# Retention mixer's entry: a written order for VectorE and ScalarE, and the values' first weight tiles requested ahead of the sums

## The chip, the cores and the metric

One NeuronCore of a Trainium2 chip runs the whole program. The metric is device microseconds of one execution. The core's engines run side by side, each through its own in-order list of instructions, and semaphores hold an instruction until its operands are there: TensorE (PE) multiplies, VectorE (DVE) and ScalarE (ACT) work on tiles of 128 partitions, GpSimd (POOL) and SyncE (SP) issue DMA transfers here, POOL those that add to what already lies in the tile.

## The reference, cut to what matters

The program is a two-layer encoder for 512 tokens of width 1024: layer 0 mixes with window and neighbourhood attention, layer 1 with retention, each followed by an MLP. The change lies at the start of layer 1's mixer:

```python
def _odd_mixer(x, norm_g, w_in, dec_f, dec_b, gn_g, w_out):
    B, S, _ = x.shape
    h = _rmsnorm(x, norm_g)
    q, k, v, g = _split(h @ w_in, ODD_SPLITS)      # 1024, 1024, 2048, 2048 columns
    q = q.reshape(B, S, RET_HEADS, RET_DK)
    k = k.reshape(B, S, RET_HEADS, RET_DK) * (RET_DK ** -0.5)
    v = v.reshape(B, S, RET_HEADS, RET_DV)
    ...
```

All of it is float32.

## The kernel before

**Precision.** A float32 operand is split into a high part (a cast, on ScalarE) and a low part (operand minus high part, on VectorE). A product is three matmuls: high by high, high by low, low by high. So every weight tile of 128x1024 (512 KB, asked for by a DMA on SP's queue) costs one cast on ScalarE and one subtraction on VectorE before TensorE can finish with it. In `load_w` (L130 on) these are L165 and L166, the tiles are called `wraw`, `whi`, `wlo`.

**The entry of the retention mixer** works on `xg`, the transposed input times the norm's gain. The division by the root mean square is done at the end, since it is a factor per token: `rq_*`, a few 128x4 operations, give it in `tok_r`; `wide` (L1691) spreads it, four transposes on TensorE (L1698) turn it, and ScalarE copies it to `rstd_b` (L1699). `deviations` holds these, and `proj_a` calls it by a hook in its second half.

`project` for the first quarter of the heads does, in this order: `proj_a` for q (two weight tiles, 48 matmuls of 512 columns), `values.combine(0)` to `(3)`, `proj_a` for k (two tiles), the start of the values. Evacuating q or k is one multiplication by `rstd_b` (VectorE, to `tmp`), a cast `qh`/`kh` (ScalarE, L1710) and a subtraction `ql`/`kl` (VectorE, L1711).

**The values** (class `Projections`, a `Strassen`) are blocked 2x2 and use seven products instead of eight, with sums of weight blocks and of input blocks. Each product is cut in two steps x = 0, 1 of one weight tile and 12 matmuls (L1509 to L1511), so steps 0 and 1 multiply by the weight block A11, steps 2 and 3 by S1 = A21 + A22, steps 4 and 5 by S2 = A11 + S1 (the addition is `sum2`, on VectorE, L1079, in place in A11's tile), steps 6 and 7 by A12, 8 and 9 by S3, and so on. `combine(i)` makes the input's combinations for a pair i of row blocks: `row` (the input by its gain, ScalarE, L1005), four operations of 256 columns to `c` (VectorE, L1011 to L1014), a cast `uh` (ScalarE, L1017) and a subtraction `ul` (VectorE, L1018). Steps 2 to 5 read all four, two in x = 0 and two in x = 1. `high(k)` and `low(k)` (L1101, L1107) make a step's weight parts, called `shi`/`slo` for every third step and `whi`/`wlo` for the others.

**Requests.** `request` asks on SP's queue for a plain block (L1074) or for the first addend of a sum (L1070); for a sum POOL then issues a second DMA that adds the second addend (L1072), once the first has landed. `ask(a, b)` issues the requests planned for steps a to b - 1. A11 and the sums share a pool of six tiles `sraw`; block combinations alternate between a tile `c` of their own and one of these.

**Order.** In the stream of steps (`stream`, two steps ahead: product of k, early calls, `high(k + 2)`, calls of `mid[k]`, `low(k + 2)`, calls of `post[k]`), DVE, ACT and PE run in the order in which the code is written (`tc.manual_schedule`). Before the stream, in `project`, a scheduler of the compiler sets each engine's order from its own estimate and from `high_priority` and `issue_after`.

Of the kernel before, what the change touches and what calls it, by code (L numbers as in the profile page):

```python
# [9 lines left out]
F32 = mybir.dt.float32  # L10
F32R = mybir.dt.float32r
AF = mybir.ActivationFunctionType
ALU = mybir.AluOpType
# [3 lines left out]
P = 128  # L17
# [15 lines left out]
def hybrid_encoder_kernel(  # L33
# [18 lines left out]
    nc = tc.nc  # L52
    mm = nc.tensor.matmul
    act = nc.scalar.activation
    V = nc.vector
# [113 lines left out]
    def proj_a(w, r0, nk, c0, xs, evac, hook=None):  # L169

        ps = [acc(), acc()]
        chunks = {}

        def weights(kb):
            if kb not in chunks:
                rows = slice(r0 + kb * P, r0 + min(kb + 4, nk) * P)
                chunks[kb] = load_w([w[rows, c0 : c0 + 256]], 4)
            return chunks[kb]

        for k, m in [(k, m) for k in range(nk) for m in range(2)]:  # L180
            if hook is not None and (k, m) == (4, 0):
                hook(0)
            hi, lo = weights(k - k % 4)
            if hook is not None and (k, m) == (4, 0):
                hook(1)
            xh, xl = xs[k]
            cs = slice(m * P, (m + 1) * P)
            mm(ps[m], hi[:, k % 4, cs], xh, start=k == 0, stop=False)  # L188
            mm(ps[m], hi[:, k % 4, cs], xl, start=False, stop=False)  # L189
            mm(ps[m], lo[:, k % 4, cs], xh, start=False, stop=k == nk - 1)  # L190
        for m in range(2):
            evac(m, ps[m])
# [770 lines left out]
    class Strassen:  # L963
# [17 lines left out]
        READS2 = ((0, 0, 1), (1, 1, -1), (0, 1, 1), (0, 0, 1), (1, 1, -1), (0, 1, 1), (1, 0, -1))  # L981
        KEPT = ("kept", "sq", "rstd_b", "sq")
        SB = 4
        CB = (("sraw", 6),)

        def __init__(self, pool, w1, w2, norm, last):
            self.pool, self.w, self.w2, self.norm, self.last = pool, w1, w2, norm, last
            self.raw, self.parts, self.ins = {}, {}, {}
            self.steps, self.base = [], {}
            for q in range(4):  # L990
                if q:
                    for u in (2 * q, 2 * q + 1):
                        self.base[1, u] = len(self.steps)
                        self.steps += [(1, u, j, 0) for j in range(7)]
                self.base[2, q] = len(self.steps)
                self.steps += [(2, q, j, x) for j in range(7) for x in range(2)]
            self.early, self.mid, self.post, self.asked = ({} for _ in range(4))
            self.hid, self.val, self.rows, self.ps = {}, {}, {}, {}
            self.requests()

        def combine(self, i):

            pool, norm = self.pool, self.norm
            y = self.tmp()
            act(y, xT[2 * i], AF.Copy, scale=norm.gain(2 * i))  # L1005
            b11, b12 = y[:, :256], y[:, 256:]
            x21, x22 = xT[2 * i + 1][:, :256], xT[2 * i + 1][:, 256:]
            g, ng = norm.gain(2 * i + 1), norm.minus_gain(2 * i + 1)
            tag, bufs = self.CB[i % len(self.CB)]
            c = pool.tile([P, 4, 256], F32, tag=tag, bufs=bufs, name="c")  # L1010
            V.tensor_tensor(c[:, 0], b11, b12, op=ALU.subtract)  # L1011
            V.scalar_tensor_tensor(c[:, 1], x22, ng, c[:, 0], op0=ALU.mult, op1=ALU.subtract)
            V.scalar_tensor_tensor(c[:, 2], x22, g, b12, op0=ALU.mult, op1=ALU.subtract)
            V.scalar_tensor_tensor(c[:, 3], x21, ng, c[:, 1], op0=ALU.mult, op1=ALU.subtract)  # L1014
            h = pool.tile([P, 4, 256], F32R, tag=f"uh{i}", name="uh")
# [41 lines left out]
        def block(self, kind, u, name, x):  # L1057
# [3 lines left out]
            r, c = u * 1024 + j * 512 + x * 256, i * 512  # L1061
            return self.w2[r : r + 256, c : c + 512].rearrange("(k p) c -> p k c", p=P)

        def request(self, kind, u, name, x):
            pl, tag, bufs = (wpool, "wraw", 3) if name in ("A12", "A22") else (self.pool, "sraw", 6)
            t = pl.tile([P, 1024], F32, tag=tag, bufs=bufs, name=tag)
            v = t[:].rearrange("p (k c) -> p k c", k=4 if kind == 1 else 2)
            self.raw[kind, u, name, x] = v
            if name[0] == "S":
                self.asked_last = nc.sync.dma_start(v, self.block(kind, u, "A21", x)).ins  # L1070
                second = self.block(kind, u, "A22" if name == "S1" else "A11", x)
                G.dma_start(v, second, accum_op=ALU.add)  # L1072
            else:
                nc.sync.dma_start(v, self.block(kind, u, name, x))  # L1074

        def sum2(self, kind, u, x=0):

# [371 lines left out]
    class Projections(Strassen):  # L1449
# [2 lines left out]

        CB = (("c", 1), ("sraw", 6))

        def __init__(self, pool, row, tiny, w, norm, done, rb, gates):
            self.pool, self.tiny, self.w, self.norm, self.done = pool, tiny, w, norm, done
            self.rb, self.gates = rb, gates
            self.tmp = row  # L1460
            self.raw, self.parts, self.ins, self.rows, self.ps = {}, {}, {}, {}, {}
# [201 lines left out]
    def odd_mixer(norm, next_norm):  # L1663
# [4 lines left out]
        late, marks = [], []  # L1668
# [6 lines left out]
        G.memset(gn_eps, GN_EPS)  # L1675

        delta = pool.tile([P, 896], F32, name="delta")
        nc.scalar.dma_start(delta, delta_d)

        rc = tok_r[:, 0]  # L1680
        rb = stat.tile([P, S], F32, tag="rstd_b", name="rstd_b")
# [1 line left out]

        def deviations(part):

            if part:
                values.ask(-99, -8)
                return
            rsqrt_small(rc, mean_square(), NB, tiny)
            wide = stat.tile([P, S], F32, tag="sq", bufs=2, name="wide")  # L1690
            V.tensor_copy(  # L1691
                wide[:].rearrange("p (t m) -> p t m", t=NB),
                rc.unsqueeze(2).to_broadcast([P, NB, P]),
            )
            pt = aux()
            for t in range(NB):
                ts = slice(t * P, (t + 1) * P)
                nc.tensor.transpose(pt[:, ts], wide[:, ts], ident)  # L1698
            nc.scalar.copy(rb, pt)  # L1699
# [7 lines left out]
        def split(src, tag, bufs, half=half):  # L1707
            h = half(tag + "h", bufs)
            l = half(tag + "l", bufs)
            marks.append(nc.scalar.copy(h, src).ins)  # L1710
            V.tensor_tensor(l, src, h.bitcast(F32), op=ALU.subtract)  # L1711
# [8 lines left out]
        class Quarter:  # L1720
# [7 lines left out]
            def project(self):  # L1728
# [12 lines left out]
                    )  # L1741
                    self.k[m] = split(t, "k", 2)

                hook = None if qt else deviations
                mark = marks[-1] if qt else None
                proj_a(w_in_o, 0, 8, qt * 256, xg, ev_q, hook)
                if qt == 0:
                    values.combine(0)
                    values.combine(1)
                    values.ask(-99, -5)  # L1750
                    values.combine(2)
                    values.combine(3)
                first_sums = values.asked_last if qt == 0 else None
                with tc.issue_after(first_sums) if qt == 0 else ExitStack():
                    proj_a(w_in_o, 0, 8, 1024 + qt * 256, xg, ev_k)
                if qt == 0:
                    values.scales(rc)
                    values.ask(-2, 1)
                    values.ask(-5, -2)
                    values.enter()  # L1760
                    return
                with tc.issue_after(mark):
                    self.load_gates(nc.scalar)

            def load_v(self):
                self.back = []
# [116 lines left out]
        with tc.tile_pool(name="odd_values", bufs=1) as first:  # L1883
# [7 lines left out]
                rb,  # L1891
                gates,
            )
            quarters[0].project()
# [137 lines left out]
```

## Time and profile before

| | us |
|---|---|
| time, median of 3 runs (lowest to highest) | 1296.97 (1296.62 to 1297.88) |
| profiled execution, its own time | 1298.3 |
| its span on the core | 1296.5 |
| PE busy | 1270.2 |
| DVE busy | 1055.6 |
| ACT busy | 824.8 |
| mean granted TensorE clock | 0.996 of full speed |

The span is what the trace covers; the time is a little longer. Busy time is a share over the whole program, so it tells which engine the rest is measured by, not what a single place costs. In timeline rows the first figure is the start in us from the span's start, the second the length; several instructions of a kind in a row are one line with xN; a bracket gives the idle time before it and what ended it. Tiles are named without numbers there.

### The profile page before, as it was taken

The numbers are of one execution on the slowest core, as the hardware profiler recorded it, in microseconds if no ns is written. First come the engines' busy times: TensorE is split into PE (matmuls) and PEld (weight loads), VectorE is DVE, ScalarE is ACT, GpSimd is POOL, SyncE is SP. The second block draws the span as 40 slices with busy tenths as digits, with TensorE's granted clock in tenths as the row PEclk, the third lists the DMA queues.
The fourth block names the chain that finished last, engine by engine and source line by source line (L and its number), as shares of the span: only waits on it lengthen the run. The fifth ranks groups of instructions, "written<-read, shape, count | busy, mean of one in ns | idle before, by whom it ended". The sixth has DMA issues, their size and how long they took to land.

```text
span 1296.5 us, 19409 instructions
## 1 busy us (share of the span) xinstructions
PE 1270.2 (98%) x7186; PEld 1115.6 (86%) x7186; DVE 1055.6 (81%) x1603; ACT 824.8 (64%) x1382; POOL 160.9 (12%) x167
## 2 busy tenths in 40 slices
PE   8999999999999999988999999999999999999998
PEld 7888978888989899866899988888888889898997
DVE  6788887879797988967888789877776788979888
ACT  4789875775756757564775575463546757466573
POOL 0222430010520111011111000000000111101100
PEclk9999999999999999998999999999999999999999
DMA  5323322668696787167899343424135787867862
GB/s 170 97 74 87 100 66 77 192 165 203 169 205 168 179 220 170 50 196 173 214 284 237 108 137 114 130 68 128 49 98 165 176 215 176 201 172 179 211 148 81
DMA packets 167071, 196.15 MB, mean 151 GB/s; under 512 B 12224, under 2 KB 124864, under 8 KB 166976
## 3 DMA queue, kind: packets, MB, share of 16 engines
q1 hardware_dynamic: 130384, 147.74, 36.9%
q0 software_dynamic: 27776, 37.75, 17.9%
q10 hardware_dynamic: 8816, 9.41, 2.3%
q8 instruction: 56, 0.92, 0.3%
q14 instruction: 39, 0.32, 0.1%
HBM read 184.39 MB, written 10.49 MB: 150 GB/s over the span
## 4 chain that ended last, share of the span: by engine, by line
PE 88%; DVE 5%; ACT 3%; DMA 2%; issue 1%; POOL 0%; ACTq 0%; SPq 0%; DVEq 0%
PE acc L1299 7%; PE acc L1315 7%; PE acc L1316 7%; PE acc L1314 7%; PE acc L1300 7%; PE acc L1301 7%; PE acc L189 6%; PE acc L188 6%; PE acc L190 6%; PE acc L1510 2%; PE acc L1511 2%; PE acc L1509 2%; PE aux L1820 1%; PE aux L1821 1%; PE aux L1822 1%; PE aux L1315 1%
## 5 line engine op out<-in xcount | busy, mean ns | idle before, releaser
L1101 ACT CAST whi<-sraw 128x1024 fp32r<-128x1024 f32 x121 | 126.8, 1049 | 82.0 <-PE acc L1316 25.2
L1107 DVE TENSOR_TENSOR wlo<-sraw,whi 128x1024 fp32r<-128x1024 f32 x121 | 147.8, 1222 | 34.0 <-ACT whi L1101 33.5
L165 ACT CAST whi<-wraw 128x1024 fp32r<-128x1024 f32 (+2 forms) x83 | 78.5, 946 | 77.5 <-PE acc L189 44.6
L166 DVE TENSOR_TENSOR wlo<-wraw,whi 128x1024 fp32r<-128x1024 f32 (+2 forms) x74 | 82.6, 1116 | 38.7 <-ACT whi L165 37.8
L1072 POOL DMA_DIRECT2D sraw<-in_w_mlp_out_dram x32 | 38.7, 1251 | 597.7 <-DMA sraw<-in_w_mlp_out_dram 411.4
L188 PE MATMUL acc<-xh,whi 128*128 128x512 f32 x272 | 106.3, 392 | 0.0
L189 PE MATMUL acc<-xl,whi 128*128 128x512 f32 x272 | 105.9, 389 | 0.0
L190 PE MATMUL acc<-xh,wlo 128*128 128x512 f32 x272 | 105.8, 389 | 0.0
L1299 PE MATMUL acc<-uh,whi 128*128 128x256 f32 x344 | 97.9, 285 | 0.4 <-ACT s L1190 0.3
L1300 PE MATMUL acc<-ul,whi 128*128 128x256 f32 x344 | 97.3, 283 | 0.0
L1301 PE MATMUL acc<-uh,wlo 128*128 128x256 f32 x344 | 97.3, 283 | 0.0
L1101 ACT CAST shi<-sraw 128x1024 fp32r<-128x1024 f32 x59 | 62.0, 1050 | 49.1 <-PE acc L1316 10.7
L1107 DVE TENSOR_TENSOR slo<-sraw,shi 128x1024 fp32r<-128x1024 f32 x59 | 72.1, 1222 | 19.4 <-ACT shi L1101 19.0
L1268 DVE SCALAR_TENSOR_TENSOR rows<-acc,tok_r,rows 128x512 f32<-128x512 f32 (+1 forms) x97 | 71.5, 740 | 1.9 <-PE acc L1316 1.9
L1107 DVE TENSOR_TENSOR wlo<-wraw,whi 128x1024 fp32r<-128x1024 f32 x46 | 56.2, 1221 | 15.0 <-ACT whi L1101 15.0
L1299 PEld LDWEIGHTS acc<-uh,whi 128*128 128x128 f32 x344 | 66.0, 192 | 1.2 <-ACT s L1190 1.2
L1300 PEld LDWEIGHTS acc<-ul,whi 128*128 128x128 f32 x344 | 66.0, 192 | 0.0
L1301 PEld LDWEIGHTS acc<-uh,wlo 128*128 128x128 f32 x344 | 66.0, 192 | 0.0
L190 PEld LDWEIGHTS acc<-xh,wlo 128*128 128x128 f32 x272 | 51.1, 188 | 10.8
L189 PEld LDWEIGHTS acc<-xl,whi 128*128 128x128 f32 x272 | 51.1, 188 | 10.4
L188 PEld LDWEIGHTS acc<-xh,whi 128*128 128x128 f32 x272 | 51.1, 188 | 10.4
L1101 ACT CAST whi<-wraw 128x1024 fp32r<-128x1024 f32 x46 | 48.3, 1050 | 11.4 <-PE acc L1316 9.0
(400 smaller groups left out, 4180.3 us busy)
## 6 DMA issues: line engine op xcount, KB each, us to landing
sraw<-in_w_mlp_out_dram SPq DMA_DIRECT2D x48, 512.0 KB
wraw<-in_w_mlp_in_dram SPq DMA_DIRECT2D x40, 512.0 KB
sraw<-in_w_mlp_in_dram SPq DMA_DIRECT2D x36, 512.0 KB
sraw<-in_w_mlp_out_dram POOLq DMA_DIRECT2D x32, 512.0 KB, 8.7
wraw<-in_w_mlp_out_dram SPq DMA_DIRECT2D x32, 512.0 KB
wraw<-in_w_in_o_dram SPq DMA_DIRECT2D x32, 512.0 KB
sraw<-in_w_mlp_in_dram POOLq DMA_DIRECT2D x24, 512.0 KB, 8.2
sraw<-in_w_in_o_dram SPq DMA_DIRECT2D x24, 512.0 KB
```

The source lines that it names most:

```text
L166: eng.tensor_tensor(lu, used, hu.bitcast(F32), op=ALU.subtract)
L188: mm(ps[m], hi[:, k % 4, cs], xh, start=k == 0, stop=False)
L189: mm(ps[m], hi[:, k % 4, cs], xl, start=False, stop=False)
L190: mm(ps[m], lo[:, k % 4, cs], xh, start=False, stop=k == nk - 1)
L1101: nc.scalar.copy(h, self.weight(k))
L1107: V.tensor_tensor(l, self.weight(k), h.bitcast(F32), op=ALU.subtract)
L1299: mm(o, h[:, i, cs], bh, start=st, stop=False, skip_group_check=True)
L1300: mm(o, h[:, i, cs], bl, start=False, stop=False, skip_group_check=True)
L1301: mm(o, l[:, i, cs], bh, start=False, stop=i == 3, skip_group_check=True)
L1314: mm(oc, bh[:, i, cs], hc, start=st, stop=False, skip_group_check=True)
L1315: mm(oc, bh[:, i, cs], lc, start=False, stop=False, skip_group_check=True)
L1316: mm(oc, bl[:, i, cs], hc, start=False, stop=end, skip_group_check=True)
```

## The change

The entry of the first quarter gets a function of its own, `project_first`, whose VectorE and ScalarE instructions are issued in the written order. `combine` is split in three (`gained`: the row; `combined`: the four operations; `combined_parts`: the cast and the subtraction), all four blocks use one tile `c`, and the three pieces are placed one by one. `deviations` runs in q's second half from `part` 2; A11 is asked for by its hook at q's second tile (`part` 3), after `raw_tile` has taken the tiles for S1. A12, S3 and so on follow k. k's casts and subtractions go into `mid[2]` and `mid[3]` of the stream, block 3 into `post[0]`, and the decay distances `delta` (448 KB) are asked for on SP's queue in step 4's `early` calls instead of on ACT's queue.

```diff
         for k, m in [(k, m) for k in range(nk) for m in range(2)]:
-            if hook is not None and (k, m) == (4, 0):
-                hook(0)
+            if hook is not None and (k, m) in ((0, 0), (4, 0)):
+                hook(2 * (k // 4))
             hi, lo = weights(k - k % 4)
-            if hook is not None and (k, m) == (4, 0):
-                hook(1)
+            if hook is not None and (k, m) in ((0, 0), (4, 0)):
+                hook(2 * (k // 4) + 1)
...
+        def gained(self, i):
+            self.y[i] = self.tmp()
+            act(self.y[i], xT[2 * i], AF.Copy, scale=self.norm.gain(2 * i))
...
-        CB = (("c", 1), ("sraw", 6))
+        CB = ("c", 1)
...
-        nc.scalar.dma_start(delta, delta_d)
...
-            if part:
-                values.ask(-99, -8)
+            if part < 2:
+                return
+            if part == 3:
+                for x in range(2):
+                    values.raw_tile(2, 0, "S1", x)
+                for x in range(2):
+                    values.request(2, 0, "A11", x)
                 return
...
+                def between(step):
+                    if step == 0:
+                        values.combined(0)
+                    elif step == 2:
+                        values.combined_parts(0)
+                        values.combined(1)
+                        for m in range(2):
+                            part("q", m)
+                        for m in range(2):
+                            parts("q", m)
+
+                proj_a(w_in_o, 0, 8, 0, xg, keep("q"), deviations)
+                E = mybir.EngineType
+                with tc.manual_schedule(engines={E.DVE, E.Activation}):
+                    for i in range(4):
+                        values.gained(i)
+                    with tc.issue_after(values.asked_last):
+                        proj_a(w_in_o, 0, 8, 1024, xg, keep("k"), between)
+                    values.ask(-99, -7)
...
+                    values.scales(rc)
+                    values.ask(-2, 1)
+                    values.ask(-7, -2)
+                    values.combined_parts(1)
+                    values.high(0)
+                    values.low(0)
+                    values.combined(2)
+                    values.high(1)
+                    values.low(1)
+                    values.combined_parts(2)
+                    for m in range(2):
+                        part("k", m)
+
+                def rest():
+                    values.combined(3)
+                    values.combined_parts(3)
+
+                values.post.setdefault(0, []).append(rest)
+                values.mid.setdefault(2, []).append(lambda: parts("k", 0))
+                values.mid.setdefault(3, []).append(lambda: parts("k", 1))
+                values.early.setdefault(4, []).append(lambda: nc.sync.dma_start(delta, delta_d))
```

What the queues and engines then hold, in three places. In the rows stand line, operation, result and operands; the numbers behind the names tell one tile from another.

SP's queue behind q's two weight tiles, before: S1's first addends (L1070), k's tiles (L144), A12 (L1074, `wraw`), A11 (L1074, `sraw`), A22, S3.

```order
L1070 DMA sraw_6243<-in_w_in_o_dram 128x2x512
L1070 DMA sraw_6246<-in_w_in_o_dram 128x2x512
L144 DMA wraw_6335<-in_w_in_o_dram 128x4x256
L144 DMA wraw_6365<-in_w_in_o_dram 128x4x256
L1074 DMA wraw_6410<-in_w_in_o_dram 128x2x512
L1074 DMA wraw_6412<-in_w_in_o_dram 128x2x512
L1074 DMA sraw_6307<-in_w_in_o_dram 128x2x512
L1074 DMA sraw_6309<-in_w_in_o_dram 128x2x512
L1074 DMA wraw_6560<-in_w_in_o_dram 128x2x512
L1070 DMA sraw_6414<-in_w_in_o_dram 128x2x512
```

The same place after; plain blocks are now L1093, first addends L1089.

```order
L1093 DMA sraw_6244<-in_w_in_o_dram 128x2x512
L1093 DMA sraw_6246<-in_w_in_o_dram 128x2x512
L144 DMA wraw_6289<-in_w_in_o_dram 128x4x256
L144 DMA wraw_6340<-in_w_in_o_dram 128x4x256
L1089 DMA sraw_6242<-in_w_in_o_dram 128x2x512
L1089 DMA sraw_6243<-in_w_in_o_dram 128x2x512
L1093 DMA wraw_6377<-in_w_in_o_dram 128x2x512
L1093 DMA wraw_6379<-in_w_in_o_dram 128x2x512
L1089 DMA sraw_6381<-in_w_in_o_dram 128x2x512
L1089 DMA sraw_6384<-in_w_in_o_dram 128x2x512
L1837 DMA delta_6180<-in_delta_dram 128x896
L1093 DMA wraw_6563<-in_w_in_o_dram 128x2x512
```

A11 (the first two rows after, the seventh and eighth before) has changed places with S1 and moved ahead of k and A12; S3 and the distances stand ahead of A22.

ScalarE from k's second weight tile to the values' first, before:

```order
L165 CAST whi_6367<-wraw_6365 128x1024
L1017 CAST uh_6292<-c_6287 128x1024
L1699 COPY rstd_b_6182<-aux_6231 128x512
L1101 CAST shi_6420<-sraw_6307 128x1024
L1710 CAST qh_6275<-tmp_6273 128x512
L1710 CAST qh_6281<-tmp_6279 128x512
L1101 CAST whi_6424<-sraw_6309 128x1024
```

The same place after:

```order
L1722 COPY rstd_b_6181<-aux_6230 128x512
L1028 CAST uh_6319<-c_6284 128x1024
L1733 CAST qh_6332<-tmp_6328 128x512
L1733 CAST qh_6336<-tmp_6330 128x512
L165 CAST whi_6342<-wraw_6340 128x1024
L1028 CAST uh_6387<-c_6323 128x1024
L1120 CAST shi_6391<-sraw_6244 128x1024
L1120 CAST whi_6400<-sraw_6246 128x1024
```

The casts of q (`qh`) stand ahead of A11's (`shi`) instead of behind it, and ahead of k's second one (`whi_6342`).

VectorE from the values' first low part on, through S1's and S2's, before:

```order
L1107 TENSOR_TENSOR slo_6421<-sraw_6307,shi_6420 128x1024
L1711 TENSOR_TENSOR kl_6404<-tmp_6401,kh_6403 128x512
L1107 TENSOR_TENSOR wlo_6425<-sraw_6309,whi_6424 128x1024
L1107 TENSOR_TENSOR wlo_6445<-sraw_6243,whi_6444 128x1024
L1107 TENSOR_TENSOR slo_6461<-sraw_6246,shi_6460 128x1024
L1079 TENSOR_TENSOR sraw_6307<-sraw_6307,sraw_6243 128x1024
L1107 TENSOR_TENSOR wlo_6482<-sraw_6307,whi_6481 128x1024
L1079 TENSOR_TENSOR sraw_6309<-sraw_6309,sraw_6246 128x1024
L1107 TENSOR_TENSOR wlo_6501<-sraw_6309,whi_6500 128x1024
```

After, from S1's first low part on (the four operations on `c_6433` and `ul_6439` are block 3):

```order
L1126 TENSOR_TENSOR wlo_6430<-sraw_6242,whi_6429 128x1024
L1018 TENSOR_TENSOR c_6433<-row_6280 128x256
L1019 SCALAR_TENSOR_TENSOR c_6433<-xT7_6158,ngv_104,c_6433 128x256
L1020 SCALAR_TENSOR_TENSOR c_6433<-xT7_6158,gv_76,row_6280 128x256
L1021 SCALAR_TENSOR_TENSOR c_6433<-xT7_6158,ngv_104,c_6433 128x256
L1029 TENSOR_TENSOR ul_6439<-c_6433,uh_6438 128x1024
L1126 TENSOR_TENSOR slo_6455<-sraw_6243,shi_6454 128x1024
L1098 TENSOR_TENSOR sraw_6244<-sraw_6244,sraw_6242 128x1024
L1734 TENSOR_TENSOR kl_6479<-tmp_6408,kh_6478 128x512
L1126 TENSOR_TENSOR wlo_6476<-sraw_6244,whi_6475 128x1024
L1098 TENSOR_TENSOR sraw_6246<-sraw_6246,sraw_6243 128x1024
L1734 TENSOR_TENSOR kl_6502<-tmp_6410,kh_6501 128x512
```

Before, all four blocks and k's first low part stand ahead of `slo_6421`; after, block 3 stands between S1's two low parts, and k's low parts between an S2 sum and its low part.

More of the change, by code (lines that the diff above doesn't have):

```diff
@@ L983, in hybrid_encoder_kernel @@
         SB = 4
-        CB = (("sraw", 6),)
+        CB = ("sraw", 6)
         def __init__(self, pool, w1, w2, norm, last):
@@ L997, in __init__, with combined @@
             self.early, self.mid, self.post, self.asked = ({} for _ in range(4))
-            self.hid, self.val, self.rows, self.ps = {}, {}, {}, {}
+            self.hid, self.val, self.rows, self.ps, self.y = {}, {}, {}, {}, {}
             self.requests()
         def combine(self, i):
-            pool, norm = self.pool, self.norm
-            y = self.tmp()
-            act(y, xT[2 * i], AF.Copy, scale=norm.gain(2 * i))
+            self.gained(i)
+            self.combined(i)
+            self.combined_parts(i)
+        def gained(self, i):
+            self.y[i] = self.tmp()
+            act(self.y[i], xT[2 * i], AF.Copy, scale=self.norm.gain(2 * i))
+        def combined(self, i):
+            pool, norm, y = self.pool, self.norm, self.y.pop(i)
             b11, b12 = y[:, :256], y[:, 256:]
@@ L1008, in combine @@
             g, ng = norm.gain(2 * i + 1), norm.minus_gain(2 * i + 1)
-            tag, bufs = self.CB[i % len(self.CB)]
+            tag, bufs = self.CB
             c = pool.tile([P, 4, 256], F32, tag=tag, bufs=bufs, name="c")
@@ L1014, in combine, with combined_parts @@
             V.scalar_tensor_tensor(c[:, 3], x21, ng, c[:, 1], op0=ALU.mult, op1=ALU.subtract)
+            self.c = c
+        def combined_parts(self, i):
+            pool, norm, c = self.pool, self.norm, self.c
             h = pool.tile([P, 4, 256], F32R, tag=f"uh{i}", name="uh")
@@ L1062, in block, with raw_tile @@
             return self.w2[r : r + 256, c : c + 512].rearrange("(k p) c -> p k c", p=P)
+        def raw_tile(self, kind, u, name, x):
+            if (kind, u, name, x) not in self.raw:
+                pl, tag, bufs = (self.pool, "sraw", 6)
+                if name in ("A12", "A22"):
+                    pl, tag, bufs = wpool, "wraw", 3
+                t = pl.tile([P, 1024], F32, tag=tag, bufs=bufs, name=tag)
+                self.raw[kind, u, name, x] = t[:].rearrange(
+                    "p (k c) -> p k c", k=4 if kind == 1 else 2
+                )
+            return self.raw[kind, u, name, x]
         def request(self, kind, u, name, x):
[L1065 to L1068, printed above, removed]
+            v = self.raw_tile(kind, u, name, x)
             if name[0] == "S":
-                self.asked_last = nc.sync.dma_start(v, self.block(kind, u, "A21", x)).ins
+                nc.sync.dma_start(v, self.block(kind, u, "A21", x))
                 second = self.block(kind, u, "A22" if name == "S1" else "A11", x)
@@ L1073, in request @@
             else:
-                nc.sync.dma_start(v, self.block(kind, u, name, x))
+                self.asked_last = nc.sync.dma_start(v, self.block(kind, u, name, x)).ins
         def sum2(self, kind, u, x=0):
@@ L1460, in __init__ @@
             self.tmp = row
-            self.raw, self.parts, self.ins, self.rows, self.ps = {}, {}, {}, {}, {}
+            self.raw, self.parts, self.ins, self.rows, self.ps, self.y = {}, {}, {}, {}, {}, {}
             self.early, self.mid, self.post, self.asked = ({} for _ in range(4))
@@ L1742, in ev_k @@
                     self.k[m] = split(t, "k", 2)
[L1744 to L1753, printed above, removed]
@@ L1754, in project, with project_first, keep, part @@
-                with tc.issue_after(first_sums) if qt == 0 else ExitStack():
-                    proj_a(w_in_o, 0, 8, 1024 + qt * 256, xg, ev_k)
-                if qt == 0:
+                mark = marks[-1]
+                proj_a(w_in_o, 0, 8, qt * 256, xg, ev_q)
+                proj_a(w_in_o, 0, 8, 1024 + qt * 256, xg, ev_k)
+                with tc.issue_after(mark):
+                    self.load_gates(nc.scalar)
+            def project_first(self):
+                self.q, self.k = [None] * 2, [None] * 2
+                ps, t = {}, {}
+                def keep(x):
+                    return lambda m, tile: ps.update({(x, m): tile})
+                def part(x, m):
+                    t[m] = tmp()
+                    if x == "q":
+                        V.tensor_tensor(t[m], ps[x, m], rb, op=ALU.mult)
+                    else:
+                        V.scalar_tensor_tensor(
+                            t[m], ps[x, m], float(np.float32(P**-0.5)), rb, op0=ALU.mult, op1=ALU.mult
+                        )
+                def parts(x, m):
+                    (self.q if x == "q" else self.k)[m] = split(t[m], x, 2)
+                def between(step):
[16 more added lines that the diff above has]
+                    values.ask(-99, -7)
+                    values.asked = {
+                        k: [key for key in keys if key[:3] != (2, 0, "A11")]
+                        for k, keys in values.asked.items()
+                    }
@@ L1757, in project @@
                     values.scales(rc)
                     values.ask(-2, 1)
[L1759 to L1763, printed above, removed]
+                    values.ask(-7, -2)
[4 more added lines that the diff above has]
+                    values.high(1)
@@ L1893, in odd_mixer @@
             )
-            quarters[0].project()
+            quarters[0].project_first()
             for hl in range(2):
```

## The prediction

> **What bounds the kernel now.** I read the page's busy times and chain first, then TensorE's waits, then stretches of the span, then the timeline of one engine after another round the longest wait.
>
> ```profile
> PE 1270.2 (98%) x7186; PEld 1115.6 (86%) x7186; DVE 1055.6 (81%) x1603; ACT 824.8 (64%) x1382; POOL 160.9 (12%) x167
> ...
> PE 88%; DVE 5%; ACT 3%; DMA 2%; issue 1%; POOL 0%; ACTq 0%; SPq 0%; DVEq 0%
> ```
>
> TensorE (PE) is the bound: time can only come out of its 26 us of idleness or out of stretches at a low clock. One wait is most of what there is to win:
>
> ```profile
> PE acc L1510 <- DVE slo L1107: 10.2, 1, 10.2
> ```
>
> It is the second matmul of the values' first product, waiting for the low part of its weight (`slo`). The stretches, with columns length, busy time of PE, PEld, DVE, ACT, POOL, granted clock, DMA share, GB/s:
>
> ```profile
> 71.50:74.00 2.50, 1.15 (x8) 0.64 (x7) 2.50 (x4) 1.44 (x3) 1.98 (x2) 1.00 0.37 108
> 578.50:582.50 4.00, 0.00 (x0) 0.00 (x0) 4.00 (x10) 1.76 (x3) 0.00 (x0) 1.00 0.00 0
> 582.50:588.50 6.00, 0.00 (x0) 0.00 (x0) 6.00 (x10) 3.78 (x5) 1.19 (x1) 0.51 0.50 125
> 588.50:593.00 4.50, 4.32 (x11) 3.42 (x12) 3.00 (x4) 0.00 (x0) 1.19 (x1) 0.52 0.90 183
> 593.00:1292.00 699.00, 698.78 (x3881) 610.25 (x3880) 570.15 (x744) 422.77 (x643) 49.97 (x40) 1.00 0.60 158
> ```
>
> Three things: in the gap VectorE (DVE) works without a pause; the clock falls to half about 4 us into the gap and stays there to about 593; from 593 to 1292 PE is never without work, so a shift of the entry is carried to the end one to one, unless something later comes late. TensorE round the gap (start, length, instruction):
>
> ```profile
> 566.06 0.39 PE L190 MATMUL acc<-xh,wlo 128*128 128x512 f32 x1
> 567.32 0.66 PE L1698 MATMUL aux<-ident,wide 128*128 128x128 f32 x4 [0.87 <-DVE wide L1691]
> ...
> 578.06 0.39 PE L1509 MATMUL acc<-shi,xh 128*128 128x512 f32 x1
> 588.68 0.80 PE L1510 MATMUL acc<-slo,xh 128*128 128x512 f32 x1 [10.23 <-DVE slo L1107]
> ...
> 592.99 0.39 PE L1511 MATMUL acc<-shi,xl 128*128 128x512 f32 x1
> 593.22 0.40 PE L1509 MATMUL acc<-whi,xh 128*128 128x512 f32 x1
> ...
> 604.38 0.39 PE L1510 MATMUL acc<-wlo,uh 128*128 128x512 f32 x1
> ```
>
> From 593.22 (first matmul of step 1) to 604.38 (second of step 5) lie 49 matmuls: 0.228 us each, 2.73 a step of 12. By starts the entry loses 567.32 - 566.06 - 0.23 = 1.03 at `wide`, 588.68 - 578.06 - 0.23 = 10.39 in the gap, and 4.31 instead of 2.28 over the ten matmuls to 592.99: 2.03. Together 13.45 us, and no change here can win more.
>
> Why `slo` is late, read from SP's, POOL's, ACT's and DVE's timelines and the page of DMA issues (last figure: us from issue to landing):
>
> ```profile
> 555.54 0.88 SPq L1070 DMA_DIRECT2D sraw<-in_w_in_o_dram  x2
> ...
> 557.58 7.99 SPq L1074 DMA_DIRECT2D wraw<-in_w_in_o_dram  x2
> 565.62 1.17 SPq L1074 DMA_DIRECT2D sraw<-in_w_in_o_dram  x2
> ```
> ```profile
> 559.82 1.23 POOL L1072 DMA_DIRECT2D sraw<-in_w_in_o_dram  x1 [2.87 <-DMA sraw<-in_w_in_o_dram]
> 561.54 1.21 POOL L1072 DMA_DIRECT2D sraw<-in_w_in_o_dram  x1 [0.49 <-DMA sraw<-in_w_in_o_dram]
> ```
> ```profile
> sraw<-in_w_in_o_dram POOLq DMA_DIRECT2D x1, 512.0 KB, 9.7
> ...
> sraw<-in_w_in_o_dram POOLq DMA_DIRECT2D x1, 512.0 KB, 12.8
> ```
> ```profile
> 562.86 1.05 ACT L165 CAST whi<-wraw 128x1024 fp32r<-128x1024 f32 x1 [2.02 <-DMA wraw<-in_w_in_o_dram]
> ...
> 566.38 1.03 ACT L165 CAST whi<-wraw 128x1024 fp32r<-128x1024 f32 x1
> ...
> 575.79 1.05 ACT L1101 CAST shi<-sraw 128x1024 fp32r<-128x1024 f32 x1 [6.57 <-DMA sraw<-in_w_in_o_dram]
> 576.74 1.14 ACT L1710 CAST qh<-tmp 128x512 fp32r<-128x512 f32 x2
> 577.78 1.04 ACT L1101 CAST whi<-sraw 128x1024 fp32r<-128x1024 f32 x1
> ```
> ```profile
> 566.85 0.42 DVE L1691 COPY wide<-tok_r 128x512 f32<-128x512 f32 x1
> ...
> 577.39 1.29 DVE L1711 TENSOR_TENSOR ql<-tmp,qh 128x512 fp32r<-128x512 f32 x2 [5.47 <-ACT qh L1710]
> ...
> 579.00 0.42 DVE L1011 TENSOR_TENSOR c<-row 128x256 f32<-128x256 f32 x1
> 579.33 0.48 DVE L1013 SCALAR_TENSOR_TENSOR c<-xT,gv,row 128x256 f32<-128x256 f32 x1
> 579.73 0.48 DVE L1012 SCALAR_TENSOR_TENSOR c<-xT,ngv,c 128x256 f32<-128x256 f32 x1
> ...
> 587.40 1.22 DVE L1107 TENSOR_TENSOR slo<-sraw,shi 128x1024 fp32r<-128x1024 f32 x1
> 588.54 0.68 DVE L1711 TENSOR_TENSOR kl<-tmp,kh 128x512 fp32r<-128x512 f32 x1
> ...
> 595.70 1.22 DVE L1079 TENSOR_TENSOR sraw<-sraw 128x1024 f32<-128x1024 f32 x1
> ```
>
> SP asks for A11 last, at 565.62. ScalarE (ACT) stands 6.57 us for it with the q casts queued behind; VectorE stands 5.47 us for those, and only then does the rest of the combination, k's parts and, last, `slo`.
>
> **The requests.** A11 takes S1's place at the head. S1 had landed there when POOL could ask for its second halves, 559.82 and 561.54; ScalarE first reads it at 572.6 (walked below), so its landing costs nothing, with 10 us of cover. k keeps its place: the first tile landed by 562.86, the second by 566.38. S1 is now asked for behind k, and its second halves wait for it. Bounds for S1's landing: not before the second k tile's neighbourhood, 564, not after the 575.79 at which A11, asked for eight microseconds later, landed; I take 566 and 567.5, an estimate from the place directly behind k. With 9.7 to 12.8 for the sums they are whole at 575.7 to 580.3, and ScalarE reaches them (below) at 578.1 and 584.4; VectorE needs the first cast only by 580.5. Hidden, with 1 to 4 us to spare. The decay distances move from ACT's queue to SP's, behind S3, ahead of A22's request; two tiles took SP 0.88, so this is about 0.4 us there, and their first reader is far off:
>
> ```profile
> L1791 DVE TENSOR_SCALAR strip<-delta,nlb x8: 675/680/682, 644.7 to 865.0; 128x896 f32<-128x896 f32 x8
> ```
>
> Nothing, then: 80 us hide it, and A22 is first cast some 40 us after its request.
>
> **The order, walked in before's microseconds.** Durations to the next instruction: 1024 columns 0.95 on ScalarE (575.79 to 576.74), 1.14 on VectorE (587.40 to 588.54; its result counts after 1.22); 512 columns 0.52 on ScalarE, 0.61 on VectorE; the four ops of a block 0.33 to 0.48 each, 1.7 where one waits for the other.
>
> The row of deviations comes sooner: block 0's ops and four small ones end at 563.2 and `wide` at 563.6. Its transposes stand 13 matmuls sooner, at 566.29 - 13 x 0.227 = 563.34: wait 0.3 instead of 1.03. k's first low part ends at 565.5 (needed about 566.1), block 0's low at 567.1, block 1's ops 568.9, q's two evacuations 570.1. Behind their casts ScalarE now does k's second cast, 570.7 to 571.7; its low ends at 573.0, some 0.2 after TensorE asks. Then block 1's low, A11's first low at 575.4, block 2's ops, A11's second low 578.2, block 2's low 579.4, k's two evacuations 580.6, S1's first low 581.75, block 3's ops 583.4, its cast 584.5 and low 585.75, S1's second low 586.9.
>
> TensorE: step 0 starts at 578.06 - 1.03 + 0.5 = 577.55 and needs its low at 577.8 (ready 575.4: the 10.39 and the clock's 2.03 go). Step 1 at 580.28 (ready 578.2), step 2 at 583.01 (581.75), step 3 at 585.74; its second matmul, wanted at 585.97, gets its low at 586.9: wait 0.9. Now VectorE is late. The S2 rounds are a ring: sum 1.22, S2's cast 1.05, behind it k's cast 0.5, k's low (on VectorE, ahead of S2's low) 0.65, S2's low 1.2: 4.6 us a round where TensorE takes 2.73. Lows at 591.5 and 596.1, two waits of 1.87. From step 6 on the sums are over: A12's low at 597.2 against 598.8. So step 5's second matmul stands at 596.1 where it stood at 604.38: **8.3 us** less; the same from the losses, 13.45 - 0.5 - 0.9 - 2 x 1.87 = 8.3.
>
> The profiled execution took 1298.3 (span 1296.5); the median of the runs, 1296.97, lies 1.33 lower. 1298.3 - 8.3 - 1.33 = **1288.7 us**. The walk's soft terms are some 15 handovers of about 0.1 and the ring twice, +-1.5.
>
> **The clock.** The new waits come three in a row. In 71.50:74.00 TensorE is busy 46% and the clock stays 1.00; it also stays 1.00 through four idle microseconds from 578.50. From 586.9 to 596.1 TensorE will have 24 matmuls, 5.5 of 9.2 us, 59%: I take a full clock. A rule speaks against it: the Trainium skill, "TensorE: Matmul & The Clock Gate", section "A second HAM failure mode: psum-queue depth-cycling", says that short pauses between groups of matmuls, if they come often enough, make the clock swing between half and full. By that rule rival C below would hold; the row of 71.50 does not bear it out.
>
> **Rivals.** B: the ring runs as in before. There the next sum followed after 3.55 us (595.70; next at 599.25):
>
> ```profile
> 599.25 1.22 DVE L1079 TENSOR_TENSOR sraw<-sraw 128x1024 f32<-128x1024 f32 x1
> ```
>
> That was without k's parts inside it; if they cost nothing, 2 x 1.05 more is won: 1286.6, and 1283.5 if all 13.45 go. Against it: k's cast and low stand inside the ring in program order. C: half clock in the new waits. A fall lasts about 10 us (582.5 to 593) at 0.43 a matmul (4.31 by ten). From 591.5: step 5's second matmul at 591.5 + 12 x 0.43 = 596.7, 0.6 late, and 11 more at 0.2 extra: 2.8, so 1291.5; from 587, about 1.1: 1289.8. D, the slower side: S1's sums land late. ScalarE's in-order cast of S1's second tile then holds all behind it, one to one beyond 584.4. Landing at 592.7 eats the whole gain; 0.2% slower needs 595.3, some 28 us after the issue at 567.5, where the two rows took 9.7 and 12.8. If both sums queue behind A12, S3 and the distances for 20 us, 3 of the 8.3 go: 1291.7. E: the first tile still waits, for k's last parts or its buffers: 1297. Against it: k's second evacuation stands behind A11's lows.
>
> **How the numbers follow.** Forecast 0.68, own range 1287.2 to 1290.2; B 0.09; C 0.12; D 0.07, of which 0.03 slower than before and 0.01 about equal; E 0.04, of which 0.01 slower. A measurement of this kernel can tell about 0.2%, 2.6 us. Faster 0.92, same 0.04, slower 0.04. The range 1286.6 to 1292.0 takes in the near ends of B, C and D and leaves out about 0.15.
>
> **What would show it.** Right: no TensorE wait near 578; waits on VectorE of about 0.9, 1.9 and 1.9 in steps 3, 4 and 5, named L1126 low parts; the clock at 1.00 all through; from about 585 before's 593 pattern, PE never waiting to the end. Wrong: a cast of S1 waiting for a DMA (D); a clock near 0.5 after 587 (C); the two rounds 3.6 apart (B); a new wait after 600, which the row 593.00:1292.00 gives no sign of.

## The result, and the profile after

| | before | after |
|---|---|---|
| median of the runs made side by side (4 each) | 1297.43 | 1290.89 |
| lowest to highest | 1296.62 to 1297.93 | 1290.38 to 1291.27 |
| profiled execution, its own time | 1298.3 | 1291.21 |
| its span | 1296.5 | 1289.4 |

The ratio is 0.995 (95% interval 0.9933 to 0.9967): 6.5 us faster, where 8.3 were forecast. From the page after, busy times, then the shares of the chain:

```profile
PE 1269.0 (98%) x7186; PEld 1114.2 (86%) x7186; DVE 1057.3 (82%) x1603; ACT 824.1 (64%) x1382; POOL 161.3 (13%) x167
...
PE 81%; DVE 8%; ACT 7%; issue 3%; DMA 1%; POOL 0%; SPq 0%; ACTq 0%; DVEq 0%
```

VectorE and ScalarE have a larger share of the chain than before: the end hangs on them for longer, though it comes sooner. TensorE's waits after (line: us in total, times, longest):

```profile
PE acc L1529 <- DVE wlo L1126: 3.3, 2, 1.7
...
PE acc L1529 <- DVE slo L1126: 0.7, 1, 0.7
PE aux L1721 <- DVE wide L1714: 0.4, 1, 0.4
```

One wait of 10.2 us has become three on the low parts of steps 3, 4 and 5. The stretches after (columns as in the prediction):

```profile
560.00:578.00 18.00, 17.52 (x79) 13.88 (x78) 15.09 (x29) 11.56 (x18) 3.76 (x4) 1.00 1.04 314
578.00:587.00 9.00, 8.71 (x39) 6.88 (x37) 7.84 (x11) 4.02 (x5) 1.06 (x1) 1.00 0.94 195
587.00:597.00 10.00, 6.31 (x25) 4.64 (x26) 6.58 (x8) 5.81 (x9) 1.19 (x1) 1.00 0.41 108
597.00:1285.00 688.00, 687.76 (x3833) 601.30 (x3832) 564.08 (x739) 416.22 (x635) 48.64 (x39) 1.00 0.60 158
```

The clock stays at 1.00 although TensorE is busy only 63% from 587 to 597, and from 597 on it stands only 0.24 us in 688, as before from 593 on (0.22 in 699). TensorE's timeline after at the places that the prediction walked through:

```profile
563.34 0.39 PE L189 MATMUL acc<-xl,whi 128*128 128x512 f32 x1
564.14 0.63 PE L1721 MATMUL aux<-ident,wide 128*128 128x128 f32 x4 [0.41 <-DVE wide L1714]
...
573.03 0.40 PE L189 MATMUL acc<-xl,whi 128*128 128x512 f32 x1
573.49 0.73 PE L190 MATMUL acc<-xh,wlo 128*128 128x512 f32 x2
574.06 0.40 PE L188 MATMUL acc<-xh,whi 128*128 128x512 f32 x1
...
578.16 0.39 PE L1528 MATMUL acc<-shi,xh 128*128 128x512 f32 x1
578.39 0.39 PE L1529 MATMUL acc<-slo,xh 128*128 128x512 f32 x1
...
587.37 0.50 PE L1529 MATMUL acc<-slo,uh 128*128 128x512 f32 x1 [0.66 <-DVE slo L1126]
...
592.04 0.50 PE L1529 MATMUL acc<-wlo,uh 128*128 128x512 f32 x1 [1.66 <-DVE wlo L1126]
592.38 0.39 PE L1530 MATMUL acc<-whi,ul 128*128 128x512 f32 x1
...
596.72 0.50 PE L1529 MATMUL acc<-wlo,uh 128*128 128x512 f32 x1 [1.66 <-DVE wlo L1126]
```

Step 0 runs from its first to its second matmul in 0.23 us where it took 10.62. The two S2 rounds, 587.37 to 592.04 and on to 596.72, are 4.67 and 4.68 us apart. The ring on VectorE and ScalarE, in the first of them:

```profile
587.23 1.22 DVE L1098 TENSOR_TENSOR sraw<-sraw 128x1024 f32<-128x1024 f32 x1
590.16 0.69 DVE L1734 TENSOR_TENSOR kl<-tmp,kh 128x512 fp32r<-128x512 f32 x1 [1.71 <-ACT kh L1733]
590.77 1.22 DVE L1126 TENSOR_TENSOR wlo<-sraw,whi 128x1024 fp32r<-128x1024 f32 x1
591.91 1.22 DVE L1098 TENSOR_TENSOR sraw<-sraw 128x1024 f32<-128x1024 f32 x1
```
```profile
588.56 1.05 ACT L1120 CAST whi<-sraw 128x1024 fp32r<-128x1024 f32 x1 [2.21 <-DVE sraw L1098]
589.52 0.61 ACT L1733 CAST kh<-tmp 128x512 fp32r<-128x512 f32 x1
```

Sum, S2's cast, k's cast, k's low, S2's low, the next sum; VectorE stands 1.71 us in it, for a cast that nobody needs yet.

To set executions side by side I use one more measure, from one matmul on line 666 (in layer 0; the first on that line after 71 us, the same one in every run) to the last one of the program, since the program's first 73 us vary. Before, then after:

```profile
72.50 0.30 PE L666 MATMUL aux<-ident,p 128*128 128x128 f32 x1 [0.62 <-DVE p L587]
```
```profile
1292.31 0.28 PE L1316 MATMUL acc<-whi,lT 128*128 128x256 f32 x1
```
```profile
72.69 0.30 PE L666 MATMUL aux<-ident,p 128*128 128x128 f32 x1 [0.83 <-DVE p L587]
```
```profile
1284.88 0.28 PE L1335 MATMUL acc<-whi,lT 128*128 128x256 f32 x1
```

1219.81 and 1212.19: 7.62 us less. I call it the inner span; below it is read in the same way from each trace. The two executions of the changed kernel differ in it by 0.10, and that arises in layer 0: from a matmul of q's, 1.7 us ahead of the transposes of `wide` (562.43 after), to the last they agree within 0.02.

### The profile page after: what moved, and what is told of

The parts are those of the page before. It is cut to its first block, busy times and chain, and to the rows that moved or that the text cites. A ratio compares the mean times of both kernels' runs of the same rounds, so it can differ in the third digit from the quotient of the medians.

```text
span 1289.4 us, 19413 instructions
## 1 busy us (share of the span) xinstructions
PE 1269.0 (98%) x7186; PEld 1114.2 (86%) x7186; DVE 1057.3 (82%) x1603; ACT 824.1 (64%) x1382; POOL 161.3 (13%) x167
## 4 chain that ended last, share of the span: by engine, by line
PE 81%; DVE 8%; ACT 7%; issue 3%; DMA 1%; POOL 0%; SPq 0%; ACTq 0%; DVEq 0%
PE acc L1333 7%; PE acc L1334 7%; PE acc L1335 7%; PE acc L189 7%; PE acc L190 7%; PE acc L188 7%; PE acc L1318 5%; PE acc L1319 5%; PE acc L1320 5%; DVE wlo L1126 1%; PE acc L1529 1%; PE acc L1530 1%; PE acc L1528 1%; PE aux L1894 1%; PE aux L1895 1%
## 5 line engine op out<-in xcount | busy, mean ns | idle before, releaser
L1120 ACT CAST whi<-wraw 128x1024 fp32r<-128x1024 f32 x46 | 48.3, 1051 | 10.2 <-PE acc L1335 8.9
```

The source lines that it names most:

```text
L1120: nc.scalar.copy(h, self.weight(k))
```

## The experiments

| run | median us (lowest to highest) | inner span |
|---|---|---|
| before | 1297.43; 1297.91, 1298.01, 1297.51 beside the later ones | 1219.81 |
| after; again as e7_after_again | 1290.89; 1290.97 (1290.33 to 1291.46) | 1212.19; 1212.29 |
| e1_old_requests | 1293.08 (1292.04 to 1293.29) | 1214.71 |
| e2_requests_only | 1293.33 (1292.74 to 1294.33) | 1215.22 |
| e3_k_parts_out | 1288.42 (1288.24 to 1289.23) | 1209.82 |
| e4_sums_early; again as e10_sums_again | 1286.43 (1286.04 to 1287.34); 1287.37 (1287.14 to 1287.47) | 1208.30; 1208.29 |
| e5_delta_on_act | 1290.14 (1289.37 to 1290.88) | 1211.61 |
| e6_all_early | 1286.55 (1286.09 to 1287.29) | 1207.69 |
| e8_best | 1285.54 (1285.44 to 1286.53) | 1207.67 |
| e9_rstd_later | 1289.67 (1289.49 to 1290.45) | 1211.55 |

My theory: the gain comes from VectorE reaching the first low part in time; the requests are needed to feed it; what is left is VectorE's arrears and the ring. Rivals: the requests alone did it; VectorE is simply short of time, whatever the order.

**The order without the requests.**

```diff
                 for x in range(2):
-                    values.raw_tile(2, 0, "S1", x)
-                for x in range(2):
-                    values.request(2, 0, "A11", x)
+                    values.request(2, 0, "S1", x)
...
-                    values.ask(-7, -2)
+                    with tc.issue_after(values.asked_last):
+                        values.ask(-7, -5)
+                    values.ask(-5, -2)
```

> The changed kernel with the requests in the old order: S1, k, A12, then A11. Theory (VectorE's written order carries the gain, the requests only feed it): A11 lands near 576 as before, ScalarE stands some 2.8 us for it and VectorE's list starts 2.2 us later from A11's first low part on; the first product still finds its low part near 578, and the 2.2 us come out as longer waits in steps 3 to 5: 1290.9 + 2.2 = 1293.1. Rival (the requests carry the gain): the ten-microsecond wait is back and the time with it, 1296 to 1297. Second rival (the requests do nothing, VectorE is late anyway): 1290.9.

1293.08, 2.1 to 2.2 more than the changed kernel, 2.5 in the inner span. ScalarE's A11 cast and VectorE's first low part in its timeline:

```profile
575.37 1.05 ACT L1120 CAST shi<-sraw 128x1024 fp32r<-128x1024 f32 x1 [2.99 <-DMA sraw<-in_w_in_o_dram]
```
```profile
576.46 1.23 DVE L1126 TENSOR_TENSOR slo<-sraw,shi 128x1024 fp32r<-128x1024 f32 x1 [2.48 <-ACT shi L1120]
```

The first product did not wait; TensorE stood 0.5 us in step 2 and 1.8 in step 3, where it had stood 0.7 in all, while the waits of steps 4 and 5 stayed as they were (1.64 and 1.66); I had expected the loss in steps 3 to 5. So the written order alone takes the ten-microsecond wait away and is worth 4.8 us, the new requests win another 2.1 to 2.5, and the rival that the requests carry the gain falls.

**The requests without the order.**

```diff
             if part:
-                values.ask(-99, -8)
+                for x in range(2):
+                    values.request(2, 0, "A11", x)
                 return
...
-                    values.ask(-99, -5)
...
+                    values.ask(-99, -7)
...
-                    values.ask(-2, 1)
-                    values.ask(-5, -2)
+                    with tc.issue_after(values.asked_last):
+                        values.ask(-2, 1)
+                    values.ask(-7, -2)
```

> The kernel before with the requests alone in the new order (A11, k, S1, A12), no written order. Theory: A11 lands near 560, ScalarE and VectorE no longer stand for it, and what is left of the wait is k's evacuations and low part, which stand ahead of the first low part: it ends near 582, so a wait of 3.7 us instead of 10.2, and the half clock does not set in: 1297.4 - 6.7 - 2.0 = 1288.7 (1290.7 if the clock falls all the same). Rival (the order on VectorE is what counts): its 11.2 us of work from 577.4 on only begin 5.5 us sooner, 1292 or more.

1293.33: 4.6 us faster than before, half of what I expected, and on the rival's side of its bound. TensorE's waits in its timeline, and stretches in and behind the gap:

```profile
567.38 0.66 PE L1699 MATMUL aux<-ident,wide 128*128 128x128 f32 x4 [1.34 <-DVE wide L1692]
...
583.19 0.79 PE L1510 MATMUL acc<-slo,xh 128*128 128x512 f32 x1 [4.70 <-DVE slo L1107]
```
```profile
578.50:581.50 3.00, 0.00 (x0) 0.00 (x0) 3.00 (x5) 0.96 (x2) 1.19 (x1) 1.00 0.26 27
581.60:588.00 6.40, 4.81 (x11) 3.79 (x12) 4.41 (x7) 1.56 (x2) 1.19 (x1) 0.50 0.81 230
```

The wait is 4.7 instead of 3.7 (both k evacuations, a cast and a low stand in line for it), the clock fell all the same, so its 2 us stay lost (the ten matmuls behind the gap, 583.19 to 587.62, took 4.43 us, 4.31 before), and the wait at `wide` is 0.5 longer. Either half of the change alone gives 4.6 to 4.8 us, since both work on the same wait: both together gave 6.5 to 7.0 beside the runs of before.

**k's parts out of the ring.**

```diff
-                values.mid.setdefault(2, []).append(lambda: parts("k", 0))
-                values.mid.setdefault(3, []).append(lambda: parts("k", 1))
+                values.mid.setdefault(6, []).append(lambda: parts("k", 0))
+                values.mid.setdefault(7, []).append(lambda: parts("k", 1))
```

> The changed kernel with k's casts and low parts moved from mid[2] and mid[3] to mid[6] and mid[7], out of the S2 rounds. Theory (the rounds are a ring of sum, cast, k's cast, k's low, low): each round falls from 4.68 to about 3.6 us, TensorE's two waits of 1.66 to about 0.6 each, 2.1 us less: 1288.8. Rival (VectorE is short of time, not of a ring): only its own 0.6 us a round go, 1.2 less: 1289.7. Rival (the waits come back at steps 8 and 9): 1290.9.

1288.42, and 2.37 less in the inner span (2.1 expected). TensorE's waits:

```profile
586.66 0.50 PE L1529 MATMUL acc<-slo,uh 128*128 128x512 f32 x1 [0.65 <-DVE slo L1126]
...
590.22 0.50 PE L1529 MATMUL acc<-wlo,uh 128*128 128x512 f32 x1 [0.54 <-DVE wlo L1126]
...
593.77 0.50 PE L1529 MATMUL acc<-wlo,uh 128*128 128x512 f32 x1 [0.53 <-DVE wlo L1126]
```

The rounds are 3.56 and 3.55 us: 1.1 less each, where VectorE's own work fell by only 0.6. That is the ring, not a shortage of VectorE's time; and steps 8 and 9 did not wait.

**The sums early.**

```diff
-                put(post, s - 2 if q else s + 1, lambda q=q: self.sum2(2, q, 0))
-                put(post, s + 1 if q else s + 2, lambda q=q: self.sum2(2, q, 1))
+                if q:
+                    put(post, s - 2, lambda q=q: self.sum2(2, q, 0))
+                put(post, s + 1, lambda q=q: self.sum2(2, q, 1))
...
                     values.combined(3)
+                    values.sum2(2, 0, 0)
                     values.combined_parts(3)
```

> As e3_k_parts_out, and both S2 sums earlier: the first one ahead of block 3's cast and low part, where VectorE stood 1.12 us, the second right behind S1's second low part. Theory: the wait in step 3 stays (0.66), those of steps 4 and 5 (1.66 each) go, and the slower matmul behind each: 3.3 to 3.6 us less than the changed kernel, 1287.4. Rival (VectorE's work alone bounds it): as e3_k_parts_out, about 1289.

1286.43, and 3.9 less than the changed kernel in the inner span, where 3.3 to 3.6 were expected: a bracket counts from the end of the matmul before, 0.39 after its start, while the next one normally starts 0.23 after it. By starts a wait of 1.66 costs 1.82, and the slow start behind it 0.11 more. One wait of the three is left:

```profile
586.13 0.50 PE L1529 MATMUL acc<-slo,uh 128*128 128x512 f32 x1 [0.65 <-DVE slo L1126]
```

**The remaining arrears.** `e6_all_early` takes k's parts out and makes the second sum early as above, and further:

```diff
                         values.combined(1)
+                    elif step == 3:
                         for m in range(2):
                             part("q", m)
...
                     values.combined(3)
+                    values.high(3)
+                    values.low(3)
                     values.combined_parts(3)
```

The stream's own calls for step 3 then fall away.

> As e4_sums_early, with k's second low part ahead of q's evacuations, and S1's second parts ahead of block 3's cast and low part, the sums behind these. Theory (VectorE is in arrears from 564 to 588 and only the order in which it pays can be chosen): the 0.35 at k's second tile and the 0.65 of step 3 go, about 0.4 comes back in step 4 since S2's first low part keeps its time: 0.6 less than e4_sums_early, 1285.8. Rival (every change of order is paid back in full): 1286.4.

By the time alone the rival held: 1286.55, as e4_sums_early in another set of runs (1286.43). The inner span is 0.61 shorter, the 0.6 expected, but the agreement is luck. Line 666's matmul starts at 72.66 here and at 71.40 in e4_sums_early, which hid the gain in the time. But the matmul of q's named above follows it after 489.54 us here and after 489.80 there, so 0.26 of the 0.61 had been won ahead of the entry, where the change does nothing. The entry gave 0.35: the wait at k's second tile is gone, as expected, but step 3's 0.65 came back in step 4 as 0.61 and not as 0.4. For step 3 the rival was right. In q's matmuls, e4_sums_early and then here, and in step 4:

```profile
561.20 0.39 PE L188 MATMUL acc<-xh,whi 128*128 128x512 f32 x1
```
```profile
562.20 0.39 PE L188 MATMUL acc<-xh,whi 128*128 128x512 f32 x1
...
589.43 0.50 PE L1529 MATMUL acc<-wlo,uh 128*128 128x512 f32 x1 [0.61 <-DVE wlo L1126]
```

**The decay distances.**

```diff
         delta = pool.tile([P, 896], F32, name="delta")
+        nc.scalar.dma_start(delta, delta_d)
...
-                values.early.setdefault(4, []).append(lambda: nc.sync.dma_start(delta, delta_d))
```

> The changed kernel with the decay distances back on ScalarE's queue at the mixer's start (0.34 us of issue there), as before the change; on SP's queue S3's two tiles and A12's second one change places with it. Theory (the distances are hidden on either queue): the same as the changed kernel, 1290.9 within 0.4. Rival (448 KB ahead of S1 in the transfers hold S1's sums back past 584.8, and with them step 3): 1 to 3 us slower. Rival (the issue on SP holds later requests): up to 0.4 faster.

> The changed kernel unaltered, beside these two on one chip: 1290.9 within 0.5, with the three waits of steps 3 to 5 at 0.7, 1.7 and 1.7 and the clock at 1.00; a wait or a half clock that only some executions have would show as another pattern.

e7_after_again came as expected: 1290.97, waits of 0.65, 1.66 and 1.66, the clock at 1.00. e5_delta_on_act took 1290.14 beside it, 0.7 less in the inner span: more than the nothing I expected, the other way than the first rival. But the compiler's scheduler had also changed ScalarE's list: block 0's cast `uh` ahead of the copy to `rstd_b`. (On VectorE it had mixed the four small `rq_*` operations with block 0's.) VectorE's low part of block 0, after and then here:

```profile
566.37 1.23 DVE L1029 TENSOR_TENSOR ul<-c,uh 128x1024 fp32r<-128x1024 f32 x1 [0.58 <-ACT uh L1028]
```
```profile
565.30 1.22 DVE L1029 TENSOR_TENSOR ul<-c,uh 128x1024 fp32r<-128x1024 f32 x1
```

So I made that swap by itself, in the changed kernel (e9) and in e4_sums_early (e8):

```diff
-            nc.scalar.copy(rb, pt)
+            turned.append(pt)
...
                         values.combined_parts(0)
+                        nc.scalar.copy(rb, turned[0])
                         values.combined(1)
```

> The changed kernel with that swap alone, distances on SP's queue as changed. Theory (what e5_delta_on_act won came from this order on ScalarE, in which its trace also differs, and not from the queue of the distances): 0.5 less than the changed kernel, 1290.4, as e5_delta_on_act. Rival (the queue of the distances won it): 1290.9.

> e4_sums_early with one swap on ScalarE: the cast of block 0 ahead of the copy to rstd_b, so that VectorE need not stand 0.58 us ahead of block 0's low part. Theory (VectorE's list is behind from 564 on, and what it saves at its start arrives at step 3): the step 3 wait of 0.65 shrinks to 0.1, 0.5 less than e4_sums_early beside it: 1285.9. Rival (it stands again for rstd_b at q's evacuations, which are next to need it): no gain.

> e4_sums_early unaltered, beside e8_best on one chip: 1286.4 within 0.4, one wait of 0.65 in step 3 and none after it.

e9 came to 1289.67, its inner span of 1211.55 to e5's 1211.61, and counted from line 666 VectorE's instructions from block 0's low part to the first S2 sum start within 0.03 us of each other in the two: the swap explains what e5 won, and the queue of the distances is worth nothing that these runs show. e10_sums_again, at 1287.37, missed the 1286.4 within 0.4 that I had put down for it, with the wait of 0.65 as expected and an inner span equal to that of e4_sums_early within 0.01; its line 666 began 1.34 later (72.74). So the 1285.54 of e8_best beside it counts for less than it seems: in the inner span it is 0.62 less. Of this some 0.37 came at k's second tile, whose wait is gone, which I had not expected, and some 0.3 in step 3, whose wait is 0.35 (0.1 expected):

```profile
585.65 0.50 PE L1529 MATMUL acc<-slo,uh 128*128 128x512 f32 x1 [0.35 <-DVE slo L1126]
```

It beats both kernels: 0.9909 of before (interval 0.9895 to 0.9922), some 12 us, and 12.1 in the inner span.

## Why the prediction was right, and where its size was off

- **The mechanism held at every step.** No wait near 578, three waits in steps 3, 4 and 5 on the named low parts, a full clock throughout, no wait to speak of from 597 on (the prediction's "about 585" was a slip: its own walk has the last wait end at 596.1). The time alone would not have told: 1290.89 lies above my own range of 1287.2 to 1290.2 and nearest to rivals C (1291.5) and D (1291.7), which the trace rules out. e1 shows that the order alone removes the wait near 578 and that the requests save 2.1 to 2.5 us more, e2 that the requests alone only halve that wait, e3 that the late rounds are a ring.
- **The walk from step 0 on came out to 0.01, in part by luck.** Forecast 577.55 to 596.1, 18.55 us; measured 578.16 to 596.72, 18.56. The ring was given 4.6 and took 4.67. By starts, as the prediction counts, the waits are 0.82, 1.82 and 1.82 (brackets 0.66, 1.66 and 1.66), against 0.9, 1.87 and 1.87: 0.2 less together. Each is followed by a matmul that starts 0.34 behind (592.04 to 592.38) instead of 0.23, which I had not counted: 0.2 more for the two within the walk.
- **First term off: the two small waits ahead of step 0.** I gave 0.5. By starts, `wide` lost 564.14 - 563.34 - 0.23 = 0.57 (0.3 forecast), k's second tile 573.49 - 573.03 - 0.23 = 0.23 and 0.11 more behind it (0.2 forecast). Together 0.9, so 0.4 of the 8.3 is missing there. The second wait comes from ScalarE's list: the walk had block 0's low part at 567.1, but it ended at 567.60, having stood 0.58 us for a cast behind the copy to `rstd_b`. With the two swapped (e9) nothing waits at k's second tile.
- **Second: what lies around the walk.** 7.85 us are left at step 5's second matmul, counted from line 666, and 7.62 at the last matmul (0.11 us of the difference is the slow start behind the last wait). Then from the last matmul to the span's end: 4.21 us before, 4.55 after, 0.35 more, which no part of the prediction considers. It is 4.21 in e2 too, and 4.55 to 4.58 in all kernels built on the changed one; these also have the distances on either queue, so that isn't it. The last output is asked for at the same place in both (1.23 and 1.22 us after the last matmul). The 0.35 lies behind it, in the program's closing sequence: most of it between two semaphore instructions of GpSimd, 0.08 us apart in the kernel before and 0.37 in the changed one. Why is open. And the profiled execution after began 0.19 later. 7.62 - 0.35 - 0.19 = 7.1, the difference of the spans.
- **Third: from the profiled execution to the median.** I took 1.33 off, since the profile before was that far above its median. After, it stands 0.32 above: 1298.3 - 7.1 - 0.32 = 1290.9. This 1.0 is half of the miss of 2.2; 0.46 of it is that the median before was taken from three runs (1296.97, with the fourth 1297.43). Part of the 1.0 is probably an offset of the single execution (line 666 starts at 72.50 there, at 71.40 to 72.74 in others), not one of the kernel, though the other executions of before left no trace to read it from; it should have gone into the range instead of the value.
- **The requests.** S1's sums were given 575.7 to 580.3 with 1 to 4 us to spare. POOL's row after and its issues' median time:

```profile
566.23 2.56 POOL L1091 DMA_DIRECT2D sraw<-in_w_in_o_dram  x2 [9.05 <-DMA sraw<-in_w_in_o_dram]
```
```profile
sraw<-in_w_in_o_dram POOLq DMA_DIRECT2D x2, 512.0 KB, 12.0
```

The two were whole at 577.0 and 580.8; ScalarE's casts of S1 start at 578.50 and 584.82. Rival D was as far off as the prediction put it.
- **The clock.** C did not occur: 1.00 in 587.00:597.00. The rule of the Trainium skill, "TensorE: Matmul & The Clock Gate", section "A second HAM failure mode: psum-queue depth-cycling", that frequent short pauses make the clock swing, did not come into play with three pauses of 0.7, 1.7 and 1.7 us; from how many on it would, no run here shows.
- **B** was wrong as the kernel stands and right as an edit: with k's parts out, the rounds are the 3.55 of before.

## What to carry to other kernels

When a long wait is removed, walk every engine's list to the place where the first one is late again, with the handovers: what is left here was not work but a ring in which an unneeded cast stood between a sum and its consumer, and moving that alone won 2.4 us. Two halves of a change that attack the same wait do not add (4.8 and 4.6 gave 6.5 to 7.0), so the worth of each shows only with the other left out. When a small edit under a scheduler moves the time, compare the lists before believing the edit: e5's 0.7 us came from a neighbour's order. And when a total agrees with the forecast, check that its parts do: e6's 0.6 did not.

## What the runs showed of the hardware that I had not expected

In the two traces that have it, the half clock comes in whole pieces. In the trace's clock record it lasted from 582.60 for 10.24 us before, and from 581.57 for 6.83 us in e2: three and two times 3.41. It fell about 4.2 and 3.1 us after TensorE had run dry, and outlasted the gap by 4.2 and 5.2 us. So the gap of 4.7 us paid no less for the matmuls behind it than the one of 10.2, and waits of 1.7 us paid nothing. In both traces the fall came 570.03 us after the record's first full clock, which is 167 such pieces. The Trainium skill, "TensorE: Matmul & The Clock Gate", section "What's actually happening", gives a free-running window of 3413 ns that doesn't start with the kernel; both lengths agree with it, and so does the varying start that follows.

The first 73 us of the program varied by 1.3 us between executions of one and the same kernel (71.40 and 72.74 at line 666 in the two runs of e4_sums_early), while the 1208 us behind them agreed within 0.01. The clock accounts for nearly all of it: its record shows the first full clock at 10.60 us in the one and at 13.28 in the other, and just there the matmuls' starts go from 0.43 us apart to 0.23. e4_sums_early, then e10_sums_again:

```profile
10.14 0.61 PE L264 MATMUL acc<-wlo,xh 128*128 128x512 f32 x1
10.57 0.42 PE L265 MATMUL acc<-whi,xl 128*128 128x512 f32 x1
10.82 0.39 PE L264 MATMUL acc<-wlo,xh 128*128 128x512 f32 x1
11.05 0.39 PE L265 MATMUL acc<-whi,xl 128*128 128x512 f32 x1
```
```profile
12.43 0.63 PE L265 MATMUL acc<-whi,xl 128*128 128x512 f32 x1
12.86 0.60 PE L263 MATMUL acc<-whi,xh 128*128 128x512 f32 x1
13.28 0.40 PE L264 MATMUL acc<-wlo,xh 128*128 128x512 f32 x1
13.52 0.40 PE L265 MATMUL acc<-whi,xl 128*128 128x512 f32 x1
```

By an estimate from these rows, 2.68 us at 0.43 instead of 0.23 us a matmul lose 1.25 of the 1.34. Differences below a microsecond were to be read from behind that stretch, not from the time.
